# Three small edits at the seam between an output projection and a memory query projection: where two reciprocals stand, how eight decode rows are split, and where an exponential table is loaded

## The chip, the core and the metric

The kernel runs on one core of one Trainium2 chip. Such a core has five engines with their own instruction queues: TensorE (PE) multiplies matrices, with the loading of its stationary operand shown apart as PEld; VectorE (DVE), ScalarE (ACT) and GpSimd (POOL) work elementwise; SyncE (SP) here only starts transfers. The metric is device time in microseconds (us) of one execution of the whole program; the time of a kernel is the median of its runs.

## The reference

One inference step of a decoder layer, for a prompt of 1024 tokens and for 8 decode tokens that use the same weights, all in float32. What matters here is the end of the first part and the beginning of the second:

```python
# 1. hybrid mixer
a = head_rms(oa) * subln * (1.0 - lam_init)          # attention heads (group A)
r = head_rms(orr) * silu(gr)                         # retention heads (group B)
x = x + concatenate([a, r]) @ w_out
# 2. memory cross-attention
h = rmsnorm(x, g)                                    # g = norm_mem_q
q = (h @ w_mq)
p = softmax((q @ mk.T) * DH_M ** -0.5)
x = x + (p @ mv) @ w_mo
# 3. squared-ReLU MLP, then a final rmsnorm
```

`rmsnorm(x, g)` is `x / sqrt(mean(x*x) + eps) * g`. The decode tokens attend to a paged cache in part 1, so their rows of `oa` come by a way of their own.

## The kernel before

**Layout.** Activations lie transposed: 128 features on the partitions, tokens along the free dimension. The token columns are 1032 = 1024 prompt tokens and 8 decode tokens (`NT:T`), cut into three blocks of `CH` = 344. Blocks 0 and 1 are called the early tokens here, block 2 (688 to 1032, with the decode tokens) the late ones. The 1024 features make 8 tiles `kt`.

**Split products.** To keep float32 accuracy each operand is split into a high part, rounded by a conversion, and a low part, the rest. A product is three matmuls: high x high, high x low and low x high (`mm3`, line 80). The activations' parts lie in `UH` and `UL` ([128, 8, 1032]); those of a weight unit of 128 x 1024 in `wh` and `wl` (`unit`, line 135): a transfer into one of three `raw` buffers, the high part by a copy on ACT (line 129), the low part by a subtraction on DVE (line 130). There are four `wh` and four `wl` buffers. `split_gain` (line 143) does the same for activations and multiplies with the norm's gain: ACT at line 145 writes `UH`, DVE at line 146 writes `UL`.

**Output projection** (`proj_residual`, line 1479). It goes through the (feature tile, token block) pairs: first all of the early tokens, then the eight blocks (ft, 2). Each pair ends with an addition of the residual on DVE (line 1507, `x2`), a square on ACT (line 1562, the last at 1513) and an addition to a sum of squares on POOL (line 1563). The sums of the late tokens collect in `third` (a `raw` buffer, shown as `ssum_o`). Contraction runs over kt 4 to 7 (retention) first, then 0 to 3 (attention). Some blocks had half of their terms done earlier.

**Decode rows.** `decode_values` is a generator whose steps are taken between those blocks. Its last step transposes the 8 decode rows of the four attention heads into the PSUM tile `tr` (shown as `dtr`) and splits them into `UH` and `UL` columns 1024 to 1032 of kt 0 to 3, one head after the other (lines 1631 to 1636). The step before normalizes the rows in `oda` (the last instruction of it is line 1627). The late-token blocks need these columns.

**Norm of the query path.** `first_rstd` (line 1645) sums the squares of the early tokens over the partitions with a matmul and takes the root on ACT (line 1651) into `rb2`. Then `x2` is split with the gain `g_mq` into `UH` and `UL` for all 8 kt, first the early tokens, then the late ones (lines 1667 to 1669). The late ones overwrite columns that the last output blocks still read.

**Query projection** (from line 1735). Two reciprocals turn the roots in `rb2` into factors (line 1738), blocks 0 and 1. Then for each of four pairs of feature tiles two weight units are made (line 1740), and six blocks (f, c) of 24 matmuls each run, each scaled by `rb2` on the way out of PSUM (line 1767). Six PSUM banks hold such blocks. After the first block, (0, 0, 0), four pinned matmuls sum `third` over the partitions (tile `rs`); a root on ACT (line 1764) and a reciprocal on DVE (line 1765) make the late tokens' factors. Behind the query projection follow the memory keys and values and the attention, whose first exponential is at line 1889.

**What sets the order.** The program is not issued in the order of its text. A planner at build time takes, on each engine, what it believes ready, earlier lines first; the order on each engine is then fixed. Two things bind it: `pin[0]` keeps matmuls in the order of the text (line 64), and `with tc.issue_after(ins):` puts those instructions of its block that run on the engine of `ins` behind `ins`, without a wait of its own.

Of the kernel before, what the change touches and what calls it, by code (L numbers as in the profile page):

```python
# [10 lines left out]
F32 = mybir.dt.float32  # L11
# [37 lines left out]
def decoder_step(ctx: ExitStack, tc: tile.TileContext, i: dict, o: dict):  # L49
# [85 lines left out]
    def unit(u, parts=None, lo_engine=None, raw=None):  # L135
        return unit_of(lambda raw: [(raw[:, :1024], i["wall"][u])], f"u{u}", parts=parts, lo_engine=lo_engine, raw=raw)
# [1444 lines left out]
    with pool("x2") as XP:  # L1581
        x2 = [XP.tile([P, T], F32, tag=f"x2_{ft}", name=f"x2_{ft}") for ft in range(8)]
        g_mq = XP.tile([P, 8], F32, tag="g_mq", name="g_mq")
        nc.sync.dma_start(g_mq, i["g_mq"])
        with pool("c") as A:
            def decode_values():
                def dt(name):
                    return PB.tile([P, 512], F32, tag="av", name=name, bufs=1)

                acc = A.tile([P, T], F32, tag="dacc", name="dacc")  # L1590
                for k in range(8):
                    raw = A.tile([P, 1024], F32, tag="draw", name=f"cv_{k}", bufs=4)
                    gather(raw, i["cache_v"], idx, k)
                    with tc.issue_after(seen["DVE"]):
                        for x in range(8):
                            c = slice(x * P, x * P + P)
                            w = at[:, x % 4, 2 * k + x // 4 : 2 * k + x // 4 + 1]
                            if k == 0:
                                nc.vector.tensor_scalar(acc[:, c], raw[:, c], w, None, ALU.mult)
                            else:  # L1600
                                nc.vector.scalar_tensor_tensor(acc[:, c], raw[:, c], w, acc[:, c], ALU.mult, ALU.add)
                    yield
                vp = dt("vrep")
                mm(vp, selg, vdec, True, True)
                pd = A.tile([P, 1024], F32, tag="draw", name="pdv_8", bufs=4)
                nc.vector.tensor_mul(
                    pd[:, :512].rearrange("p (a v) -> p a v", v=P), vp.rearrange("p (a v) -> p a v", v=P),
                    at[:, :, 16:17].to_broadcast([P, 4, P]),
                )
                nc.vector.tensor_add(acc[:, :512], acc[:, :512], pd[:, :512])  # L1610
                yield

                with tc.issue_after(seen["PE"]):
                    op = dt("dop")
                    mm(op[:8, :], selgt, acc[:, 0:512], True, True)
                    mm(op[32:40, :], selgt, acc[:, 512:1024], True, True)
                    od2 = A.tile([P, 1024], F32, tag="draw", name="oda", bufs=4)
                    oda, sqd = od2[:8, 0:512], od2[:8, 512:1024]
                    nc.scalar.copy(oda, op[32:40, :])
                    nc.vector.tensor_add(oda, oda, op[:8, :])  # L1620
                    nc.vector.tensor_mul(sqd, oda, oda)
                    s4 = A.tile([8, 4], F32, tag="ds4", name="ds4")
                    nc.vector.tensor_reduce(s4, sqd.rearrange("p (h v) -> p h v", h=4), AX.X, ALU.add)
                    r4 = A.tile([8, 4], F32, tag="dr4", name="dr4")
                    rsqrt_small(r4, s4, 4, 1.0 / P, 8)
                    odv = oda.rearrange("p (h v) -> p h v", h=4)
                    nc.vector.tensor_mul(odv, odv, r4.unsqueeze(2).to_broadcast([8, 4, P]))
                yield
                yield
                with tc.issue_after(seen["PE"]):  # L1630
                    tr = dt("dtr")
                    for h in range(4):
                        nc.tensor.transpose(tr[:, h * 8 : h * 8 + 8], oda[:, h * P : h * P + P], ident[:8, :8])
                    odT = tr[:, :32].rearrange("p (k c) -> p k c", k=4)
                    for h in range(4):
                        split_gain(odT[:, h, :], subln8, h, NT, T, gcol=0)
                yield


            ssum = A.tile([P, T], F32, tag="ssum", name="ssum2")  # L1640
            early_tokens, late_tokens = slice(0, 2 * CH), slice(2 * CH, T)

            rb2s = []

            def first_rstd():
                rb2s.append(G.tile([P, T], F32, tag="rb2", name="rb2"))
                for c, (tag, n) in enumerate((("acc", 2), ("av", 1))):
                    cs = slice(c * CH, c * CH + CH)
                    f = PB.tile([P, 512], F32, tag=tag, name=f"rs_2_{c}", bufs=n)[:, :CH]
                    mm(f, ones.to_broadcast([P, P]), ssum[:, cs], True, True)  # L1650
                    nc.scalar.activation(rb2s[0][:, cs], f, AF.Sqrt, scale=1.0 / D, bias=half[:, 1:2])

            third = proj_residual(
                A, out_bank, U_OUT, OUT_KT, lambda ft: i["xT"][:, ft, :], lambda ft: x2[ft], ssum, "o", [us_out[x] for x in range(4)], decode_values(),
                [(ft, c) for ft in range(4) for c in range(2)] + [(4, 1), (7, 0)],
                lambda x: [
                    G.tile([P, 1024], F32R, tag="wl", name="wlo_3", bufs=RING) if (nm, x) == ("wl", 7)
                    else A.tile([P, 1024], F32R, tag=f"{nm}{x}", name=f"{nm}o_{x}") for nm in ("wh", "wl")
                ],
                first_rstd, ahead=len(OUT_EARLY), early=early_out, stage=([(4, 2)], [(5, 2), (6, 2)]), halved=OUT_HALVES,  # L1660
            )
            rb2 = rb2s[0]
            for ft in range(8):
                nc.gpsimd.dma_start(X2[ft], x2[ft])
        bc_ps.close()

        for lo, hi in ((0, 2 * CH), (2 * CH, T)):
            for kt in range(8):
                split_gain(x2[kt][:, lo:hi], g_mq, kt, lo, hi)

    pd_st = ExitStack()

    with pool("d") as A:
# [59 lines left out]
                    )  # L1733

        qm, dec = [], iter(())
        for c in range(2):
            cs = slice(c * CH, c * CH + CH)
            nc.vector.reciprocal(rb2[:, cs], rb2[:, cs])
        for pr in range(4):
            us = [unit(U_MQ + 2 * pr + x) for x in range(2)]  # L1740
            for f in range(2):
                qm.append(A.tile([P, T], F32, tag=f"qm{2 * pr + f}", name=f"qm_{2 * pr + f}"))

            late = [(0, 2), (1, 2)]
            rest = [(0, 0), (0, 1), (1, 0), (1, 1)]
            for f, c in late + rest if pr else rest + late:
                q = qm[2 * pr + f]
                cs = slice(c * CH, c * CH + CH)
                ps = PS.tile([P, 512], F32, tag="acc", name=f"mq_{pr}_{f}_{c}", bufs=6)
                pin[0] = (pr, f, c) == (0, 0, 0)  # L1750
                mm3(
                    ps[:, :CH],
                    [
                        (us[kt // 4][0][:, (kt % 4) * 256 + f * P : (kt % 4) * 256 + f * P + P],
                         us[kt // 4][1][:, (kt % 4) * 256 + f * P : (kt % 4) * 256 + f * P + P],
                         UH[:, kt, cs], UL[:, kt, cs])
                        for kt in range(8)
                    ],
                )
                if pin[0]:  # L1760
                    f = dt("rs_3")[:, :CH]
                    for x in range(2):
                        mm(f, ones.to_broadcast([P, P]), third[:, x * CH : x * CH + CH], x == 0, x == 1)
                    nc.scalar.activation(f, f, AF.Sqrt, scale=1.0 / D, bias=half[:, 1:2])
                    nc.vector.reciprocal(rb2[:, late_tokens], f)
                    pin[0] = False
                nc.vector.scalar_tensor_tensor(q[:, cs], ps[:, :CH], -1.0 / 16.0, rb2[:, cs], ALU.mult, ALU.mult)
                if c == 2:
                    nc.gpsimd.tensor_copy(qdm[:, 2 * pr + f, :], q[:, NT:])
                if (f, c) == (1, 2) and pr % 2:  # L1770
                    for _ in dec:
                        pass
                    dec = dec_scores(pr // 2)
                    continue
                for _ in range(3 if pr == 3 else 1):
                    next(dec, None)
# [984 lines left out]
```

## Time and profile before

| | |
|---|---|
| runs, median (lowest to highest) | 1479.63 us (1478.55 to 1484.31), 3 runs |
| profiled execution | 1479.72 us |
| its span, first to last instruction | 1478.0 us |
| mean granted clock of TensorE | 0.997 |
| loads of an activation table, whole span | 6, of 1.28 us each |

In the views of the trace a row of a timeline is: start and length in us, engine, line, operation, tile written <- tiles read, shape, count; a bracket gives how long the engine had been idle before and who released it. `UL<-x,g_mq,UH` is a low part of `x2`, `UL<-dtr,subln,UH` one of the decode rows, `rb<-rb` a reciprocal of the factors. Matmuls overlap: each lasts 0.32 us here, and one starts every 0.16 us. Idle time of an engine other than the bound one costs nothing by itself.

### The profile page before, as it was taken

To read this page: it belongs to the slowest core of one execution; us is meant where nothing else is said; L and a number is where in the kernel's file an instruction comes from. 1 tells how busy PE (TensorE), PEld (TensorE's weight loads), DVE (VectorE), ACT (ScalarE), POOL (GpSimd) and SP (SyncE) were. 2 spreads that over 40 slices of the span, in tenths; PEclk is the share of its full clock that TensorE was granted. 3 is DMA by queue.
4 is the path that set the end of the run, shared out by engine and by line. 5 is a ranking of instruction groups with operands and counts; after the bars stand their busy time and mean duration, and the time that the engine had idled before them with its cause. 6 is when DMAs were issued, how large, how long until landed. Compare 5 with 4: busy or idle time off the path is not lost.

```text
span 1478.0 us, 28131 instructions
## 1 busy us (share of the span) xinstructions
PE 1456.1 (99%) x11013; PEld 1400.9 (95%) x11013; DVE 1109.3 (75%) x2266; ACT 679.5 (46%) x1329; POOL 314.9 (21%) x345
## 2 busy tenths in 40 slices
PE   9999999999999999999999999999999999999998
PEld 7899779999889899989999999999999999999997
DVE  7666536888868765657877978888888888787876
ACT  7443435666542531257536534333434443343454
POOL 0034433122204621205022000000001311110380
PEclk9999999999999999999999999999999999999999
DMA  7255738216957175564582434334446674536273
GB/s 291 66 188 176 205 64 191 72 34 170 276 162 278 76 214 175 156 201 113 190 284 72 158 131 153 142 129 158 158 144 217 237 250 144 172 102 193 80 130 116
DMA packets 129833, 238.98 MB, mean 162 GB/s; under 512 B 13606, under 2 KB 80987, under 8 KB 129572
## 3 DMA queue, kind: packets, MB, share of 16 engines
q1 hardware_dynamic: 91354, 170.66, 36.1%
q0 software_dynamic: 27472, 46.93, 11.8%
q10 hardware_dynamic: 10874, 19.60, 3.5%
q8 instruction: 86, 1.41, 0.4%
q14 instruction: 47, 0.39, 0.1%
HBM read 171.13 MB, written 58.92 MB: 156 GB/s over the span
## 4 chain that ended last, share of the span: by engine, by line
PE 88%; DVE 6%; DMA 2%; ACT 2%; issue 1%; POOL 0%; SPq 0%; DVEq 0%; ACTq 0%
PE dn L2404 19%; PE Z L2236 9%; PE qkp L75 6%; PE Y L2236 6%; PE X L2236 6%; PE pr_m L75 6%; PE mq L75 6%; PE pr_o L75 4%; PE grp L75 3%; PE sp L75 2%; PE mk L75 2%; PE mv L75 2%; PE av L75 1%; PE mpv L75 1%; PE vap_z L524 1%; PE vrp_z L524 1%
## 5 line engine op out<-in xcount | busy, mean ns | idle before, releaser
L2404 PE MATMUL dn<-UH,wd 128*128 128x258 f32 (+1 forms) x1800 | 325.2, 283 | 1.5 <-ACT wd L2380 0.9
L2404 PEld LDWEIGHTS dn<-UH,wd 128*128 128x128 f32 x1800 | 278.6, 189 | 2.1 <-ACT wd L2380 1.0
L2404 PE MATMUL dn<-UL,wd 128*128 128x258 f32 x900 | 254.2, 282 | 0.0
L2404 PEld LDWEIGHTS dn<-UL,wd 128*128 128x128 f32 x900 | 170.0, 189 | 0.1
L2538 DVE TENSOR_TENSOR c<-c,dn 128x258 f32<-128x258 f32 (+1 forms) x217 | 88.7, 416 | 36.9 <-PE dn L2404 34.5
L2262 ACT ACTIVATE hq<-r 128x258 f32<-128x258 f32 x128 | 53.6, 420 | 119.2 <-DVE r L2261 119.2
L2236 PE MATMUL Z<-T_h,wu 128*128 128x258 f32 x512 | 98.2, 284 | 0.0
L2236 PE MATMUL X<-UH,wu 128*128 128x258 f32 x512 | 97.5, 282 | 0.0
L2380 ACT CAST wd<-raw_d 128x512 fp32r<-128x512 f32 x96 | 58.7, 619 | 78.9 <-PE dn L2404 74.1
L2044 ACT CAST wu<-raw_up 128x512 fp32r<-128x512 f32 x96 | 59.0, 615 | 60.0 <-PE Z L2236 50.0
L2373 ACT CAST UH<-raw_h 128x1032 fp32r<-128x1032 f32 x56 | 58.7, 1055 | 53.8 <-PE dn L2404 27.8
L2236 PEld LDWEIGHTS Z<-T_h,wu 128*128 128x128 f32 x512 | 81.4, 189 | 0.2 <-DVE u L2290 0.2
L2236 PEld LDWEIGHTS X<-UH,wu 128*128 128x128 f32 x512 | 81.4, 189 | 0.0
L2374 DVE TENSOR_TENSOR UL<-raw_h,UH 128x1032 fp32r<-128x1032 f32 x56 | 73.6, 1315 | 8.5 <-ACT UH L2373 8.5
L2381 DVE TENSOR_TENSOR wd<-raw_d,wd 128x512 fp32r<-128x512 f32 x96 | 72.1, 758 | 9.8 <-ACT wd L2380 9.6
L2273 POOL DMA_DIRECT2D HT<-ht x32 | 17.2, 536 | 292.4 <-DVE ht L2272 291.9
L129 ACT CAST wh_u<-raw_u 128x1024 fp32r<-128x1024 f32 x43 | 44.7, 1048 | 61.3 <-PE mq L75 39.0
L2236 PE MATMUL Z<-T_l,wu 128*128 128x258 f32 x256 | 72.4, 283 | 0.0
L2236 PE MATMUL X<-UL,wu 128*128 128x258 f32 x256 | 72.3, 283 | 0.0
L2045 DVE TENSOR_TENSOR wu<-raw_up,wu 128x512 fp32r<-128x512 f32 x96 | 64.7, 687 | 3.6 <-ACT wu L2044 3.6
L130 DVE TENSOR_TENSOR wl_u<-raw_u,wh_u 128x1024 fp32r<-128x1024 f32 x39 | 50.4, 1305 | 19.3 <-ACT wh_u L129 19.1
L75 PE MATMUL mq<-UH,wl_u 128*128 128x344 f32 x192 | 61.5, 320 | 2.1 <-DVE wl_u L130 2.1
(615 smaller groups left out, 4674.7 us busy)
## 6 DMA issues: line engine op xcount, KB each, us to landing
raw_u<-in_wall SPq DMA_DIRECT2D x49, 512.0 KB
HT<-ht POOLq DMA_DIRECT2D x32, 516.0 KB, 3.0
raw_h<-HT SPq DMA_DIRECT2D x32, 516.0 KB
raw_up<-in_wall SPq DMA_DIRECT2D x32, 512.0 KB
raw_d<-in_wall SPq DMA_DIRECT2D x32, 512.0 KB
HQ<-hq ACTq DMA_DIRECT2D x32, 387.0 KB
raw_h<-HQ SPq DMA_DIRECT2D x24, 516.0 KB
cmk<-in_cmk SPq DMA_DIRECT2D x16, 512.0 KB
```

The source lines that it names most:

```text
L75: pinned(nc.tensor.matmul(out, l, r, start=start, stop=stop))
L130: (lo_engine or nc.vector).tensor_sub(wl[:, :n], raw[:, :n], wh[:, :n].bitcast(F32))
L2044: nc.scalar.copy(w[:, :512], src)
L2045: nc.vector.tensor_sub(w[:, 512:], src, w[:, :512].bitcast(F32))
L2236: pinned(nc.tensor.matmul(ps, l, r[:, k, :], start=first and k == 0 and x == 0, stop=k == 3 and x == 2, skip_group_check=True))
L2262: nc.scalar.activation(h[:, PLACE[quad], :], r, AF.Square)
L2373: nc.scalar.copy(h, rv)
L2374: nc.vector.tensor_sub(l, rv, h.bitcast(F32))
L2380: nc.scalar.copy(w[:, :512], src)
L2381: nc.vector.tensor_sub(w[:, 512:], src, w[:, :512].bitcast(F32))
L2404: pinned(nc.tensor.matmul(ps[:, part], l, r[:, k, cq], start=first and k == 0 and x == 0, stop=k == 3 and x == 2, skip_group_check=True))
L2538: nc.vector.tensor_add(y, y, ps)
```

## The change

Three places are edited.

1. The decode rows: the four pairs of split instructions (one for each head) become one ACT and one DVE instruction over 4 x 8 columns. The DVE instruction is remembered as `seen["odT"]`, and of the early-token splits the DVE low parts of kt 4 to 7 are put behind it.
2. The two reciprocals of `rb2` move from ahead of the first weight units to behind them: behind the DVE low part of the second unit.
3. Right behind the root of the late tokens' sums, on ACT, a one-column exponential of a constant is written to a spare column of `third`. Its result is not used; it makes the exponential table the loaded one from there on.

```diff
@@ decode_values, last step
                     odT = tr[:, :32].rearrange("p (k c) -> p k c", k=4)
-                    for h in range(4):
-                        split_gain(odT[:, h, :], subln8, h, NT, T, gcol=0)
+                    nc.scalar.activation(UH[:, 0:4, NT:T], odT, AF.Copy, scale=subln8[:, 0:1])
+                    nc.vector.scalar_tensor_tensor(
+                        UL[:, 0:4, NT:T], odT, subln8[:, 0:1], UH[:, 0:4, NT:T].bitcast(F32), ALU.mult, ALU.subtract)
+                    seen["odT"] = nc.cur_bb.bb.instructions[-1]
                 yield
@@ splits of x2
         for lo, hi in ((0, 2 * CH), (2 * CH, T)):
             for kt in range(8):
-                split_gain(x2[kt][:, lo:hi], g_mq, kt, lo, hi)
+                with tc.issue_after(seen["odT"]) if not lo and kt > 3 else nullcontext():
+                    split_gain(x2[kt][:, lo:hi], g_mq, kt, lo, hi)
@@ query projection
         qm, dec = [], iter(())
-        for c in range(2):
-            cs = slice(c * CH, c * CH + CH)
-            nc.vector.reciprocal(rb2[:, cs], rb2[:, cs])
         for pr in range(4):
             us = [unit(U_MQ + 2 * pr + x) for x in range(2)]
+            if pr == 0:
+                seen["DVE"] = nc.cur_bb.bb.instructions[-1]
+                with tc.issue_after(seen["DVE"]):
+                    for c in range(2):
+                        cs = slice(c * CH, c * CH + CH)
+                        nc.vector.reciprocal(rb2[:, cs], rb2[:, cs])
...
                     nc.scalar.activation(f, f, AF.Sqrt, scale=1.0 / D, bias=half[:, 1:2])
+                    with tc.issue_after(nc.cur_bb.bb.instructions[-1]):
+                        nc.scalar.activation(third[:, 2 * CH : 2 * CH + 1], half[:, 0:1], AF.Exp)
                     nc.vector.reciprocal(rb2[:, late_tokens], f)
```

## The prediction

> **What bounds the kernel now.** Read in this order: the head of the page, the waits of PE, then the timelines of PE, DVE and ACT around the two waits that this change touches.
>
> ```profile
> span 1478.0 us, 28131 instructions
> PE 1456.1 (99%) x11013; PEld 1400.9 (95%) x11013; DVE 1109.3 (75%) x2266; ACT 679.5 (46%) x1329; POOL 314.9 (21%) x345
> ```
>
> TensorE bounds the whole span, so a microsecond counts only where PE stood idle. The waits of PE, whole span (who waited, for whom, us in total, times, longest):
>
> ```profile
> PE mq L75 <- DVE wl_u L130: 2.1, 1, 2.1
> ...
> PE pr_o L75 <- DVE UL L146: 1.4, 1, 1.4
> ```
>
> The reader is to see how small the stake is. PE's idle time in the whole span is 1478.0 - 1456.1 = 21.9 us, and the two waits around the change hold 2.1 + 1.4 of it.
>
> The first place, by the timelines of PE, ACT and DVE (start, length; in brackets the idle time before and its releaser):
>
> ```profile
> 499.74 0.90 PE L75 MATMUL pr_o<-UH,wh_u 128*128 128x344 f32 x4 [0.36 <-ACT UH L145]
> ...
> 502.51 0.43 PE L75 MATMUL pr_o<-UL,wh_u 128*128 128x344 f32 x1 [1.40 <-DVE UL L146]
> ```
> ```profile
> 499.42 0.27 ACT L145 ACTIVATE UH<-dtr,subln 128x8 fp32r<-128x8 f32 x1 [1.32 <-PE dtr L1633]
> 502.49 0.27 ACT L145 ACTIVATE UH<-dtr,subln 128x8 fp32r<-128x8 f32 x1 [2.80 <-DVE UL L146]
> ```
> ```profile
> 496.56 0.68 DVE L1627 TENSOR_TENSOR oda<-oda,dr 8x512 f32<-8x512 f32 x1 [0.73 <-POOL dr L141]
> 497.17 5.15 DVE L146 SCALAR_TENSOR_TENSOR UL<-x,g_mq,UH 128x688 fp32r<-128x688 f32 x6
> 502.25 0.21 DVE L146 SCALAR_TENSOR_TENSOR UL<-dtr,subln,UH 128x8 fp32r<-128x8 f32 x1
> ```
>
> ACT takes the first high part of the decode rows at 499.42, released by their transposes, and ends it at 499.69; but DVE is inside six low parts of the early tokens (5.15 us) and reaches the first decode low part only at 502.25. The last product blocks of the output projection need that low part.
>
> The second place is the start of the query products. DVE, then ACT, then PE:
>
> ```profile
> 511.30 2.29 DVE L1738 RECIPROCAL rb<-rb 128x344 f32<-128x344 f32 x1
> 513.51 0.45 DVE L1507 TENSOR_TENSOR x<-pr_o,x 128x344 f32<-128x344 f32 x1
> 513.88 2.29 DVE L1738 RECIPROCAL rb<-rb 128x344 f32<-128x344 f32 x1
> ...
> 517.62 1.22 DVE L130 TENSOR_TENSOR wl_u<-raw_u,wh_u 128x1024 fp32r<-128x1024 f32 x1
> 518.76 2.72 DVE L146 SCALAR_TENSOR_TENSOR UL<-x,g_mq,UH 128x344 fp32r<-128x344 f32 x2
> 521.41 0.50 DVE L1507 TENSOR_TENSOR x<-pr_o,x 128x344 f32<-128x344 f32 x1
> 521.83 2.52 DVE L146 SCALAR_TENSOR_TENSOR UL<-x,g_mq,UH 128x344 fp32r<-128x344 f32 x5
> 524.27 2.35 DVE L130 TENSOR_TENSOR wl_u<-raw_u,wh_u 128x1024 fp32r<-128x1024 f32 x2
> ```
> ```profile
> 512.61 1.05 ACT L129 CAST wh_u<-raw_u 128x1024 fp32r<-128x1024 f32 x1
> ...
> 516.52 0.58 ACT L145 ACTIVATE UH<-x,g_mq 128x344 fp32r<-128x344 f32 x1 [1.97 <-PE pr_o L75]
> ...
> 521.94 0.49 ACT L1513 ACTIVATE ssum_o<-x 128x344 f32<-128x344 f32 x1 [1.24 <-DVE x L1507]
> ```
> ```profile
> 519.62 0.32 PE L75 MATMUL mq<-UH,wh_u 128*128 128x344 f32 x1
> ...
> 525.54 0.42 PE L75 MATMUL mq<-UH,wl_u 128*128 128x344 f32 x1 [2.14 <-DVE wl_u L130]
> ...
> 527.22 1.32 PE L75 MATMUL rs<-ssum_o,ones 128*128 128x344 f32 x4
> ```
>
> And one row of the chain of work that ended last, for the pace of a query product, 44.64 / 284 = 0.157 us:
>
> ```profile
> 558.49 44.64 PE mq L75 x284
> ```
>
> Both weight high parts exist by 513.66 (the second is the row of 512.61), but DVE spends 4.58 us on two reciprocals and takes the low parts at 517.62 and 524.27. The second low part frees PE at 525.54.
>
> **The change part by part.** The sum is made against the profiled execution, 1479.72 us (span 1478.0 and 1.72 around it); the median of the runs shown is 1479.63.
>
> *Decode rows.* Four ACT and four DVE instructions of 8 columns become one each of 32 columns. The wide pair is not in the trace. For ACT, the nearest rows are 0.27 us at 8 columns and 0.58 at 344, so 32 columns lie between; I take 0.30. For DVE, the rows are 0.21 at 8 columns and 0.45 for an addition of 344 from PSUM; I take 0.26. The chain is then: high part 499.42 to 499.72, low part about 499.76 to 500.02. On DVE the planner must now put low parts 4 to 7 behind this. Ahead of it stand only low parts 2 and 3: 0 and 1 ran before the normalization at 496.56, and the six of 497.17 are 2 to 7. At 5.15 / 6 = 0.86 us each, two end at 498.9; DVE is free when the high part arrives. PE restarts at 499.74 as before, has 7 products that use only high parts (to 501.11, which is 502.51 less 1.40), and the low part comes 1.1 us before they are done. The 0.36 wait stays, the 1.40 wait goes: **-1.40 us** (between -1.0, should the row of 0.45 apply and the planner change the fill, and -1.76). The price is four low parts, 3.4 us, moved from 498.9 to about 500.0 to 503.4. Nothing on PE reads them before the query products at 518; next on DVE is the addition that began at 504.87, due 1.40 earlier, at 503.5. They fit, with 0.1 us over. An overrun would cost only the addition's start, which frees a PSUM bank, not PE's operand; I price it at nothing.
>
> *Reciprocals behind the first weights.* All that follows arrives 1.40 earlier: the second high part of the weights ready at 512.26 and the first before it, PE at the query products at 518.22. Between the additions DVE has only the two weight low parts (1.22 each) to do: the early low parts are done, and the late-token ones cannot start before 515.1, since their high parts wait for PE (row 516.52). So the first is done by about 512.3 and the second by 513.5 to 515, at the latest after one addition. PE needs the second low part first about 14 products into the query block, 14 x 0.157 = 2.2 us after 518.22, at 520.4. Cover: 5 us. The wait of 2.14 goes: **-2.14 us**. The reciprocals, 4.58 us, then run around 515 to 524, among eight late low parts of about 0.50 each. Who waits for them: the scaling of query block 0, which in PSUM holds one of six banks; at 24 x 0.157 = 3.8 us a block PE doesn't lack a bank for 22 us. Queued behind a reciprocal is also the addition of the last output block (row 521.41), whose square closes the sums that the pinned products at 527.22 read. With both stalls gone PE gets there at about 523.7; before, the sums stood at 522.43, and 1.40 earlier is 521.0. One reciprocal in between, 2.29, makes it 523.3: still in time. I price it at nothing, with 0 to 2.3 as bounds should both stand in front (521.0 + 4.58 - 523.7 = 1.9, and a POOL addition).
>
> *Table load behind the roots.* The ACT rows:
>
> ```profile
> 528.58 0.52 ACT L1764 ACTIVATE rs<-rs,half 128x344 f32<-128x344 f32 x1 [4.73 <-PE rs L75]
> 533.85 1.05 ACT L129 CAST wh_u<-raw_u 128x1024 fp32r<-128x1024 f32 x1 [4.75 <-DMA raw_u<-in_wall]
> ```
>
> and 120 us later, at the first exponentials:
>
> ```profile
> 650.63 1.28 ACT L1889 ACT_TABLE_LOAD   x1
> 652.55 0.45 ACT L1889 ACTIVATE ms<-ms,mmn 128x256 f32<-128x256 f32 x1 [0.64 <-DVE mmn L1885]
> ```
>
> Added: one load of 1.28 and an activation of one column (0.27 by the 8-column row, nearest) after 529.10, inside 4.75 us in which ACT waits for a weight transfer. Removed: the load at 650.63. It ended at 651.91 and ACT then waited 0.64 for DVE, so its removal moves nothing: **0** (bounds: 0 and -0.64, if DVE were re-ordered too). The new activation writes a spare column of the tile that holds the third sums. That tile is one of the three raw weight buffers, so its next transfer on SP's queue starts after the new write, some 2 us later than the pinned products would let it; but those run 3.5 earlier, so it is no later than now, and 0.
>
> The page ScalarE: Activation LUTs of the Trainium skill (What ACT_TABLE_LOAD costs) adds a drain of about 1.38 us to the load. By it the first exponential could not have started before 653.29 and the removal would be worth some 0.7 us, an estimate from that page; the trace has it at 652.55, 0.64 after the load, so the measurement decides against it and the sum stays.
>
> **Sum:** -1.40 - 2.14 + 0 = -3.54; 1479.72 - 3.54 = **1476.2 us**, which is 0.24% less. About 0.5% (7.4 us) is what a measurement of this kernel can tell from no change. Behind 525 the other engines follow PE's buffer releases and nothing of a fixed time stands in the list of PE's waits, so I take the gain to be kept to the end.
>
> **The rivals.**
>
> *Only one wait goes, chance 0.17.* The order on each engine is planned when the program is built, and the late low parts rank ahead of the weights, as the row of 521.83 before 524.27 shows. If the planner keeps the second weight low part behind them, only 1.40 is won: 1478.3. If it is the decode rows that stay late, 1477.6. Against it: late low parts can't start until about 515.1.
>
> *The clock comes too, chance 0.13.* Granted clock by windows (us; busy times; PEclk is the first number after POOL):
>
> ```profile
> 525.54:529.00 3.46, 3.46 (x18) 3.06 (x19) 1.60 (x2) 0.42 (x1) 0.32 (x1) 1.00 0.91 232
> 654.46:656.42 1.96, 0.01 (x2) 0.04 (x1) 1.56 (x5) 1.89 (x8) 0.00 (x0) 1.00 0.41 161
> 656.40:660.50 4.10, 4.08 (x22) 3.97 (x22) 3.19 (x8) 1.10 (x2) 0.00 (x0) 0.59 0.00 2
> ```
>
> The wait of 1.96 before 656.42 was followed by 4.1 us at 0.59, a loss of 4.10 x 0.41 = 1.7; the wait of 2.14 before 525.54 wasn't. If work shifted by 3.5 us escapes that dip, the time is 1476.2 - 1.7 = 1474.5; with the 0.64 of the table, 1473.9. The Trainium skill, TensorE: Matmul & The Clock Gate (The HAM clock gate), has the clock halve after an idle window of about 3.4 us, counted by a free-running window; by it no wait here is long enough and this rival would be void. The dip after 1.96 us speaks against that rule.
>
> *The gain is given back later, chance 0.10.* 3.5 us of earlier arrival meets a transfer, or the planner orders DVE worse before the first exponentials, where one more wait like 1.96 with its dip costs 3.7: 1479.9.
>
> *Slower, chance 0.08: the last output addition behind the reciprocals.* Suppose DVE does all it can before that addition: from about 515.1 the second weight part (1.22), both reciprocals (4.58), eight late low parts (4.0) and the third weight part (1.2). It then ends at 515.1 + 11.0 + 0.5 = 526.6 and its square at 527.1, while PE reaches the pinned products at 522.0 if it has no fill products (518.22 + 3.8). The wait is 5.1 us, and a dip like the one above comes with it: 1476.2 + 5.1 + 1.7 = 1483.0. It decides from a wait of 3.54 us on (addition ended after 525.05), or 1.84 if the clock dips. For it: a reciprocal is the longest DVE instruction there, and this addition already ran 1.8 us late behind other DVE work (PE's output block ended at 519.62, the addition began at 521.41). Against: it ranks ahead of the reciprocals whenever it is ready.
>
> **How the numbers follow.** The forecast has 0.52: both waits gone, 1475 to 1477.5. With one wait gone (1477.6 to 1478.3) and the clock (1473.9 to 1474.5) that is 0.82, so the range must reach from 1473.9 to 1478.3; the bounds of the costs (0.64 of the table and 0.36 of the first wait below; 2.3 of the pinned products above) widen it to **1473.0 to 1480.0**. Faster by over 0.5% means below 1472.2: only more than all priced gains, 0.05. Slower by over 0.5%, above 1487.1, takes more than the slow rival: 0.04. Within 0.5%: 0.91.
>
> **What would show it.** Right: on DVE two (not six) early low parts stand between the normalization and one decode low part near 500; no wait of PE for UL; both weight low parts before either reciprocal; no wait of mq for wl_u; a table load near 526 and none before the first exponential. Wrong: PE idle before the products of ssum_o (the pinned ones), late low parts ahead of the weights, or a new PE wait after 530 that eats 3.5 us.

## The result, and the profile after

The changed kernel takes 1472.90 us, the median of 8 runs (1471.88 to 1475.55), against 1480.17 for the kernel before in the same session (8 runs, 1478.55 to 1484.31). The ratio is 0.9951, with a 95% interval from 0.9939 to 0.9963: 7.3 us less, between 5.5 and 9.0. Forecast were 3.5 us less, 1476.2, with a range that ended at 1473.0. The head of the page after:

```profile
span 1473.4 us, 28129 instructions
PE 1455.7 (99%) x11013; PEld 1401.0 (95%) x11013; DVE 1107.9 (75%) x2263; ACT 679.7 (46%) x1327; POOL 314.4 (21%) x345
```

PE is as busy as before to 0.4 us; what fell is its idle time, from 21.9 to 17.7 us. The waits of PE, whole span:

```profile
PE dn L2412 <- DVE c L2546: 3.0, 2, 2.4
...
PE pr_o L75 <- ACT UH L1635: 0.4, 1, 0.4
...
PE mtr L78 <- DVE me L1901: 0.2, 1, 0.2
```

Both waits that the prediction wanted gone are gone. The third row is the surprise: the wait at the first transposes of the attention weights (tile `mtr`), 2.0 us before, is 0.2. (Most of the row at the top is one wait of 2.4 us at 1188 us, in the last projection. The clock dips behind it, so this span is only 4.6 shorter than before. A second profile of the same kernel, below, has neither, and a span of 1469.4.)

The decode rows in the timelines of ACT, DVE and PE:

```profile
499.24 0.29 ACT L1635 ACTIVATE UH<-dtr,subln 128x32 fp32r<-128x32 f32 x1 [1.03 <-PE dtr L1633]
```
```profile
494.91 0.68 DVE L1627 TENSOR_TENSOR oda<-oda,dr 8x512 f32<-8x512 f32 x1 [1.15 <-POOL dr L141]
495.52 0.92 DVE L146 SCALAR_TENSOR_TENSOR UL<-x,g_mq,UH 128x688 fp32r<-128x688 f32 x1
496.36 0.50 DVE L1507 TENSOR_TENSOR x<-pr_o,x 128x344 f32<-128x344 f32 x1
496.79 2.61 DVE L146 SCALAR_TENSOR_TENSOR UL<-x,g_mq,UH 128x688 fp32r<-128x688 f32 x3
499.56 0.25 DVE L1636 SCALAR_TENSOR_TENSOR UL<-dtr,subln,UH 128x32 fp32r<-128x32 f32 x1 [0.16 <-ACT UH L1635]
499.72 2.88 DVE L146 SCALAR_TENSOR_TENSOR UL<-x,g_mq,UH 128x688 fp32r<-128x688 f32 x3
```
```profile
499.57 0.74 PE L75 MATMUL pr_o<-UH,wh_u 128*128 128x344 f32 x3 [0.38 <-ACT UH L1635]
```

DVE is idle when the wide high part ends, takes the wide low part at once, and PE keeps only its wait of 0.38.

The start of the query products, DVE, then ACT and PE:

```profile
509.88 1.23 DVE L130 TENSOR_TENSOR wl_u<-raw_u,wh_u 128x1024 fp32r<-128x1024 f32 x1 [0.81 <-ACT wh_u L129]
511.03 0.51 DVE L1507 TENSOR_TENSOR x<-pr_o,x 128x344 f32<-128x344 f32 x1
511.45 1.54 DVE L130 TENSOR_TENSOR wl_u<-raw_u,wh_u 128x1024 fp32r<-128x1024 f32 x1
512.92 0.50 DVE L1507 TENSOR_TENSOR x<-pr_o,x 128x344 f32<-128x344 f32 x1
513.34 2.29 DVE L1746 RECIPROCAL rb<-rb 128x344 f32<-128x344 f32 x1
515.55 0.45 DVE L1507 TENSOR_TENSOR x<-pr_o,x 128x344 f32<-128x344 f32 x1
515.92 2.28 DVE L1746 RECIPROCAL rb<-rb 128x344 f32<-128x344 f32 x1
518.13 0.45 DVE L1507 TENSOR_TENSOR x<-pr_o,x 128x344 f32<-128x344 f32 x1
```
```profile
520.34 0.47 ACT L1513 ACTIVATE ssum_o<-x 128x344 f32<-128x344 f32 x1
...
523.44 1.28 ACT L1772 ACT_TABLE_LOAD   x1
524.73 0.20 ACT L1772 ACTIVATE ssum_o<-half 128x1 f32<-128x1 f32 x1
```
```profile
521.55 1.32 PE L75 MATMUL rs<-ssum_o,ones 128*128 128x344 f32 x4
```

Both weight low parts are done at 512.99, the reciprocals fill DVE behind them, and the last output addition follows the second reciprocal; its square ends at 520.81, 0.74 before PE comes to the pinned products, so PE loses nothing. The table load stands where it was put.

**Where the third gain comes from.** At the first exponentials the program is not changed, but the planned order of ACT is. In the kernel before (its first exponential, 652.55, is shown in the prediction) ACT, DVE and PE go on thus:

```profile
653.82 0.45 ACT L1889 ACTIVATE ms<-ms,mmn 128x256 f32<-128x256 f32 x1 [0.69 <-DVE mmn L1885]
```
```profile
651.84 0.68 DVE L1885 TENSOR_REDUCE mmn<-ms 128x2 f32<-128x512 f32 x1
...
654.50 0.69 DVE L1885 TENSOR_REDUCE mmn<-ms 128x2 f32<-128x512 f32 x1 [0.34 <-PE ms L75]
655.11 0.38 DVE L1891 RECIPROCAL msm<-msm 128x2 f32<-128x2 f32 x2
655.79 1.66 DVE L1893 TENSOR_SCALAR me<-ms,msm 128x256 f32<-128x256 f32 x4 [0.30 <-DVE msm L1891]
```
```profile
656.42 0.74 PE L78 MATMUL mtr<-ident,me 128*128 128x128 f32 x4 [1.96 <-ACT ms L1889]
```

and in the changed kernel:

```profile
648.17 0.45 ACT L1897 ACTIVATE ms<-ms,mmn 128x256 f32<-128x256 f32 x1 [2.19 <-DVE mmn L1893]
...
648.77 0.45 ACT L1897 ACTIVATE ms<-ms,mmn 128x256 f32<-128x256 f32 x1
```
```profile
647.46 0.68 DVE L1893 TENSOR_REDUCE mmn<-ms 128x2 f32<-128x512 f32 x1
...
649.37 0.17 DVE L1899 RECIPROCAL msm<-msm 128x2 f32<-128x2 f32 x1
```
```profile
650.25 0.74 PE L78 MATMUL mtr<-ident,me 128*128 128x128 f32 x4 [0.17 <-DVE me L1901]
```

The first score block has two halves, and its transposes need both. Before, the exponential at 653.82 is the first half of the second block (it waits for that block's minimum), and DVE takes a third minimum, which waits for PE, ahead of the reciprocals. After, both halves of the first block stand in a row. From the start of the first minimum (`mmn`) to that of the transposes it is 4.58 us before and 2.79 after.

The planned order of ACT's instructions, as the two programs have it (ms_0 is the first block, ms_1 the second; an x2 means both halves in a row):

```
before, ACT in order         changed, ACT in order
L1889 ACT_TABLE_LOAD         L1897 ACTIVATE ms_0  x2
L1889 ACTIVATE ms_0          L1897 ACTIVATE ms_1  x2
L1889 ACTIVATE ms_1          L1913 CAST mph_0
L1889 ACTIVATE ms_0
L1889 ACTIVATE ms_1
L1889 ACTIVATE ms_2  x2
L1905 CAST mph_0
```

### The profile page after: what moved, and what is told of

Its sections match the earlier page's. It is cut to its first block, busy times and chain, and to the rows that moved or that the text cites. A ratio compares the mean times of both kernels' runs of the same rounds, so it can differ in the third digit from the quotient of the medians.

```text
span 1473.4 us, 28129 instructions
## 1 busy us (share of the span) xinstructions
PE 1455.7 (99%) x11013; PEld 1401.0 (95%) x11013; DVE 1107.9 (75%) x2263; ACT 679.7 (46%) x1327; POOL 314.4 (21%) x345
## 4 chain that ended last, share of the span: by engine, by line
PE 88%; DVE 5%; DMA 2%; ACT 2%; issue 1%; POOL 0%; ACTq 0%; SPq 0%; DVEq 0%
PE dn L2412 20%; PE Z L2244 9%; PE qkp L75 6%; PE Y L2244 6%; PE X L2244 6%; PE mq L75 6%; PE pr_m L75 6%; PE pr_o L75 5%; PE grp L75 3%; PE sp L75 2%; PE mv L75 2%; PE mk L75 1%; PE av L75 1%; PE mpv L75 1%; PE vap_z L524 1%; PE vrp_z L524 1%
## 5 line engine op out<-in xcount | busy, mean ns | idle before, releaser
L2402 POOL TENSOR_TENSOR raw_d<-raw_d,raw_d 128x512 f32<-128x512 f32 x16 | 22.1, 1384 | 197.0 <-DVE raw_d L2398 145.3
```

## The experiments

Two theories at first. A: each edit pays at its own place, and the table edit pays at the first exponentials through the planned order. B: the wait of `mtr` went because everything arrives earlier. The first four kernels do one edit alone, or leave one out.

**The decode rows alone.**

Before, with the first edit:

```diff
-                    for h in range(4):
-                        split_gain(odT[:, h, :], subln8, h, NT, T, gcol=0)
+                    nc.scalar.activation(UH[:, 0:4, NT:T], odT, AF.Copy, scale=subln8[:, 0:1])
...
-                split_gain(x2[kt][:, lo:hi], g_mq, kt, lo, hi)
+                with tc.issue_after(seen["odT"]) if not lo and kt > 3 else nullcontext():
+                    split_gain(x2[kt][:, lo:hi], g_mq, kt, lo, hi)
```

> Before with the first edit alone: one wide split of the decode rows, four early low parts put behind it. Theory A (each edit pays at its own place, and the table edit pays at the first exponentials through the order planned there): the wait of pr_o for UL, 1.4 us, goes and PE reaches the first query product 1.4 to 1.7 us earlier; the wait of mtr for the exponentials stays near 2.0, with its dip of the clock; about -1.5 us in all. Theory B (the wait of mtr went because everything arrived earlier): mtr's wait shrinks here too, and the gain is over 3 us.

**The reciprocals alone.**

Before, with the second edit:

```diff
-        for c in range(2):
-            cs = slice(c * CH, c * CH + CH)
-            nc.vector.reciprocal(rb2[:, cs], rb2[:, cs])
...
+            if pr == 0:
+                seen["DVE"] = nc.cur_bb.bb.instructions[-1]
+                with tc.issue_after(seen["DVE"]):
...
+                        nc.vector.reciprocal(rb2[:, cs], rb2[:, cs])
```

> Before with the second edit alone: the two reciprocals behind the second weight low part. Theory A: the wait of mq for wl_u, 2.1 us, goes, that of pr_o for UL stays at 1.4, mtr's stays near 2.0 with its dip; -2.1 to -2.6 us. Theory B: mtr's wait shrinks with the earlier arrival, and the gain is over 4 us.

**The table edit alone.**

Before, with the third edit:

```diff
+                    with tc.issue_after(nc.cur_bb.bb.instructions[-1]):
+                        nc.scalar.activation(third[:, 2 * CH : 2 * CH + 1], half[:, 0:1], AF.Exp)
```

> Before with the third edit alone: the one-column exponential behind the root of the late sums. The planned order of the first exponentials already differs from before (both halves of the first block in a row). Theory A: mq's and pr_o's waits stay (2.1 and 1.4), mtr's wait falls from 2.0 to about 0.2 and the clock does not dip behind it; -3.3 us (1.8 and 1.6). Theory B: nothing arrives earlier, so mtr's wait stays near 2.0; 0 us.

**Without the table edit.**

The changed kernel, less the third edit:

```diff
-                    with tc.issue_after(nc.cur_bb.bb.instructions[-1]):
-                        nc.scalar.activation(third[:, 2 * CH : 2 * CH + 1], half[:, 0:1], AF.Exp)
```

> The changed kernel without the third edit: both other edits, the table loaded at the first exponential as before. Theory A: mq's and pr_o's waits gone, mtr's stays near 2.0, with or without a dip; -3.7 to -4.2 us against before. Theory B: mtr's wait falls as in the changed kernel; about -7 us.

What they and the later runs gave. The ratios are against runs of the kernel before on the same chip, with 95% intervals. The other columns are differences of starts in each kernel's one profile, in us: from the first decode transpose (`dtr`) to the first query product, from there to the decode transpose at the first scores (`dtp_m`), from the first minimum to the first transposes, and the wait of PE there.

| kernel | ratio | dtr to query | query to scores | mmn to mtr | wait of mtr |
|---|---|---|---|---|---|
| before | 1 | 20.65 | 129.14 | 4.58 | 1.96 |
| changed | 0.9951 (0.9939 to 0.9963) | 18.99 | 126.60 | 2.79 | 0.17 |
| decode rows alone | 0.9986 (0.9978 to 0.9995) | 19.01 | 131.46 | 4.16 | 2.08 |
| reciprocals alone | 0.9979 (0.9971 to 0.9988) | 20.66 | 126.59 | 4.17 | 1.55 |
| table edit alone | 0.9984 (0.9975 to 0.9992) | 20.24 | 131.26 | 2.79 | 1.13 |
| without the table edit | 0.9966 (0.9953 to 0.9979) | 19.01 | 126.61 | 4.23 | 1.60 |
| before, exponentials ordered | 0.9985 (0.9974 to 0.9996) | 20.65 | 129.16 | 3.06 | 0.44 |
| changed, old exponential order | 0.9955 (0.9941 to 0.9969) | 19.01 | 126.76 | 3.86 | 1.34 |
| without the table edit, ordered | 0.9946 (0.9931 to 0.9961) | 19.01 | 126.61 | 3.06 | 0.44 |
| changed, again | 0.9948 (0.9933 to 0.9962) | 19.02 | 126.61 | 2.79 | 0.30 |
| without the reciprocals | 0.9976 (0.9966 to 0.9985) | 19.01 | 129.51 | 2.80 | 0.17 |

Each edit has its own column, and the columns do not mix: the first is 19.0 only where the decode rows are split wide, the second 126.6 to 126.8 only where the reciprocals stand behind, and the chain is 2.8 with the table edit and 4.2 to 4.6 without it unless the exponentials are ordered by hand. The first column varies from run to run as well: over the four profiles of before that there are in the end it is 20.21, 20.65, 20.67 and 22.02. The 20.21, like the 20.24 with the table edit alone, has a wait of 0.9 us at `pr_o` in place of 1.4; the 22.02 has a dip of the clock.

In times the three alone give 2.1, 3.1 and 2.4 us (0.14, 0.21 and 0.16% of 1480), together 7.6, against 7.3 of the whole. Theory A holds. Of B little is left: the table edit alone, with nothing earlier, has the short chain, and both other edits together leave a wait of 1.60. That wait did move from 1.96 to 1.55 and 1.60 with the orders of ACT and DVE unchanged, by as much as the chain shrank (4.58 to 4.17 and 4.23). Why the chain shrank stays open, so a share of B is not shown. A's number for the table edit's wait, 0.2, was missed too: it is 1.13 in that run, with the same chain, because a weight transfer had come late and DVE began the first minimum later. Two of A's gains were short too, though inside the intervals: the reciprocals alone gave 3.1 us (1.8 to 4.3) where A had at most 2.6, and the kernel without the table edit 5.0 (3.1 to 7.0) where A had at most 4.2. And the second column of the first and third kernels is 2.2 larger than before's, which neither theory foresaw; that is the clock, below.

Is it the order, or the load itself that no longer stands in front? Two kernels part them.

**The order without moving the load.**

The kernel before, in the function that makes the scores:

```diff
             for x in range(2):
-                nc.scalar.activation(sp[:, x, :], sp[:, x, :], AF.Exp, bias=mn[:, x : x + 1], scale=-1.0,
-                                     accum_out=sm[:, x : x + 1])
+                with tc.issue_after(seen["exp"]) if (h, tp, x) in ((0, 0, 1), (0, 1, 0), (0, 1, 1)) else nullcontext():
+                    nc.scalar.activation(sp[:, x, :], sp[:, x, :], AF.Exp, bias=mn[:, x : x + 1], scale=-1.0,
+                                         accum_out=sm[:, x : x + 1])
+                if h == 0:
+                    seen["exp"] = nc.cur_bb.bb.instructions[-1]
```

> Before with none of the three edits, but with the four exponentials of the first two score blocks put in the order of the text (first block's two halves, then the second's); the table is still loaded ahead of the first of them. If the order is what the table edit bought: the chain from the first minimum (mmn) to the first transposes (mtr) falls from 4.6 us to 2.8 to 3.0, as in the run with the table edit alone (2.79), the load stays hidden ahead of it, and the gain is that of the table edit alone, 1.5 to 2.5 us. If the load itself is what cost: the chain stays above 4 us and the time that of before.

Its ACT and PE rows:

```profile
650.03 1.28 ACT L1890 ACT_TABLE_LOAD   x1
652.09 0.45 ACT L1890 ACTIVATE ms<-ms,mmn 128x256 f32<-128x256 f32 x1 [0.78 <-DVE mmn L1885]
```
```profile
654.43 0.74 PE L78 MATMUL mtr<-ident,me 128*128 128x128 f32 x4 [0.44 <-DVE me L1896]
```

The load still stands ahead of the first exponential and ends, at 651.31, 0.78 us before it; the wait of PE falls to 0.44 all the same, and the kernel gains 2.2 us (0.6 to 3.8).

**The old order without the load.**

The changed kernel, where the second half of block (0, 0) is held back; `exp` makes one exponential and remembers it, `finish` the reciprocals and products behind them:

```diff
...
+            if (h, tp) == (0, 0):
+                exp(0)
+                seen["rest"] = exp, finish
+            elif (h, tp) == (0, 1):
+                with tc.issue_after(seen["exp"]):
+                    exp(0)
+                exp_0, finish_0 = seen["rest"]
+                with tc.issue_after(seen["exp"]):
+                    exp_0(1)
+                with tc.issue_after(seen["exp"]):
+                    exp(1)
+                finish_0()
+                finish()
...
```

> The changed kernel, its table load moved as there, but the four exponentials forced into the order that before has (first block's first half, second block's first half, first block's second half, second block's second half). If the order is the cause: the chain from mmn to mtr is 0.6 to 1.8 us longer than the 2.79 of the changed kernel, the wait of mtr comes back at 0.8 to 2.0 us, and the kernel is 0.7 to 2 us slower than the changed one. If the load is the cause: 2.8 and no wait.

```profile
650.98 0.74 PE L78 MATMUL mtr<-ident,me 128*128 128x128 f32 x4 [1.34 <-DVE me L1904]
```

Without any load in the way the wait is back at 1.34 and the chain 1.07 longer. Only ACT's order is forced here; on DVE the third minimum stays behind the first block's products. So 1.07 us is the part of ACT's order. The third minimum ahead of the reciprocals, as in before, is likely the rest, but no run moved it alone. In time its median is 1.5 us above that of the changed kernel in the same session, but the two intervals overlap widely, so here the profile decides, not the times.

**Both other edits, with the exponentials ordered by hand and the load unmoved.**

The changed kernel, less the third edit, and with the exponentials chained as above:

```diff
-                        nc.scalar.activation(third[:, 2 * CH : 2 * CH + 1], half[:, 0:1], AF.Exp)
...
+                with tc.issue_after(seen["exp"]) if (h, tp, x) in ((0, 0, 1), (0, 1, 0), (0, 1, 1)) else nullcontext():
...
```

> The changed kernel without the third edit, but with the exponentials of the first two score blocks in the order of the text. If the order is all that the third edit buys: chain 2.8 to 3.0, wait of mtr under 0.5, time within 1 us of the changed kernel, about -7 us against before. If the load costs too: between the kernel without the third edit (-5.0) and the changed one.

It is not to be told from the changed kernel: 1472.94 us against 1472.44 for the next one in the same session. Beyond the order nothing of the third edit is seen. No run beat the changed kernel by more than its interval.

**The changed kernel again.** Nothing is edited.

> The changed kernel once more, unaltered. Its waits of PE around the three edits are as in its first profile (none for UL, none for wl_u, mtr 0.2), -7.3 us against before. If the dips of the granted clock belong to fixed places of the program, they lie at 1188 us again; if they fall where a wait meets a free-running window, they lie elsewhere or are absent.

The waits around the three edits are those of the first profile (`mtr` 0.30). The dip of the clock that the first had at 1188 us is absent, and so is the wait of 2.4 us ahead of it.

**The kernel before again, three times, and the second edit left out.** The three are unedited; the fourth is the changed kernel with:

```diff
+        for c in range(2):
+            cs = slice(c * CH, c * CH + CH)
+            nc.vector.reciprocal(rb2[:, cs], rb2[:, cs])
...
-            if pr == 0:
-                seen["DVE"] = nc.cur_bb.bb.instructions[-1]
...
-                        nc.vector.reciprocal(rb2[:, cs], rb2[:, cs])
```

> Before, unaltered, a second profile, for the clock alone. The three places sum to 5.8 us, the measured gain is 7.3. If the rest is dips of the granted clock that follow the two longest waits removed or shortened (mq for wl_u 2.1, mtr 2.0), then repeated profiles of before show a dip behind one of the two in about half of the cases, each worth 1.5 to 2.2 us, and not always behind the same one. If dips have nothing to do with these waits, they lie elsewhere here, as often as in the changed kernel.

> The same, third profile of before: a dip behind mq's or mtr's wait in about half of the cases.

> The same, fourth profile of before: a dip behind mq's or mtr's wait in about half of the cases.

> The changed kernel without the second edit: decode rows and table edits, reciprocals ahead of the weights. By the places: the wait of mq stays at 2.1 to 2.4 (first query product to first memory scores 129.1 us, or 131.3 with a dip of the clock), transposes to first query product 19.0, chain to mtr 2.8 us; 3.3 us under before in all. If the second edit changes the other two places, one of these numbers differs.

Windows from the restart of PE behind `mtr` in the second, third and fourth profile of before, then in the kernel with the decode rows alone (busy times as before; the granted clock is the first number behind POOL's):

```profile
658.63:662.83 4.20, 4.20 (x22) 4.07 (x23) 3.17 (x8) 1.10 (x2) 0.00 (x0) 0.60 0.02 6
```
```profile
655.52:659.32 3.80, 3.80 (x23) 3.67 (x24) 3.17 (x8) 1.10 (x2) 0.00 (x0) 0.67 0.03 6
```
```profile
660.23:664.07 3.84, 3.84 (x22) 3.71 (x23) 3.17 (x8) 1.10 (x2) 0.00 (x0) 0.67 0.03 6
```
```profile
655.57:658.29 2.72, 2.72 (x22) 2.59 (x23) 2.43 (x7) 1.39 (x4) 0.00 (x0) 1.00 0.01 3
```

The same 22 or 23 matmuls take 3.8 to 4.2 us in place of 2.7. From the first `mtr` to the first product of the next kind (`mpv`) it is 6.00 us in each of the four profiles of before and 4.46 to 4.50 in the ten others, so the dip costs 1.5 us each time. In all four profiles of before (the first is in the prediction) the clock dips behind this wait. It does not after 2.08 us of the same wait in the last row. Behind the wait of `mq`, which is 2.1 to 2.4 us in the eight profiles that have it, the clock dips in three (1.4 us in one of before, 2.2 in the kernels with the decode rows and the table edit alone), and behind the 1.4 us of `pr_o` in one profile of before (22.02 in place of 20.65 us in the first column's stretch). Of the 15 dips inside the spans of the 14 profiles that makes eight; one stands behind the wait at 1188 us, and six lie elsewhere (391.85 and 425.98 in the fourth profile of before, 390.84 and 424.97 without the table edit, 769.12 with the reciprocals alone, 775.54 with the table edit alone). So "about half", expected for the waits of `mq` and `mtr` in before, was not a good number: one of the two had a dip in all four profiles.

The stretches above are wider than a dip. The clock record has only full and half speed, and every one of the 15 dips lasts 3.41 us at half speed. In each profile the changes of the clock lie whole multiples of this length apart (before: 657.13, 660.54 and 1472.91, the last 238 lengths of 3.413 us after the second). Windows laid on these marks tell the cases apart; two are of the first profile of before, then two of the kernel with the decode rows alone:

```profile
653.72:657.13 3.41, 1.46 (x13) 1.15 (x12) 2.67 (x9) 2.54 (x10) 0.00 (x0) 1.00 0.49 163
657.13:660.54 3.41, 3.41 (x19) 3.41 (x18) 2.46 (x6) 1.10 (x2) 0.00 (x0) 0.50 0.00 0
```
```profile
651.54:654.95 3.41, 1.95 (x17) 1.75 (x15) 3.03 (x9) 2.70 (x10) 0.00 (x0) 1.00 0.96 326
654.95:658.36 3.41, 2.79 (x23) 2.69 (x24) 3.12 (x10) 1.98 (x6) 0.00 (x0) 1.00 0.02 10
```

In before the wait of 1.96 us, 654.46 to 656.42, lies whole in one window, and the next has half the clock. With the decode rows alone the wait of 2.08, 653.49 to 655.57, is cut at 654.95, and no dip follows. Over the 14 profiles, from the first mark to the last instructions, all eight windows in which PE stood idle for 1.95 us or more were followed by a dip, and none of the five with 1.5 to 1.9; the five waits of `mq` without a dip were all cut by a mark. The other seven dips follow windows with 0.26 to 1.46 us idle; what made those stays open. If the marks fall anywhere with equal chance, a wait of 1.96 us lies whole in a window in (3.41 - 1.96) / 3.41 of the cases, some four in ten. By this estimate four of four is luck, and the mean price of the dip at `mtr` is 0.6 us and not 1.5.

Leaving out the second edit gives 3.6 us (2.2 to 5.0), with the places at 1.64 + 1.79 = 3.4, and the other two places are as in the changed kernel.

## Why the prediction was wrong

**The decode rows: right, and slightly short.** The wide pair took 0.29 and 0.25 us against 0.30 and 0.26; the low part was ready at 499.81, and the wait of 1.40 went. The stretch shrank by 1.64, not 1.40. A wait in the list begins at the modelled end of a matmul, 0.16 us after the next could have started, and the product behind the first one starts 0.26 us later, not 0.16 (502.51 and 502.77 in before); so each wait costs some 0.25 us more than its row. One statement was wrong without harm: not two but four early low parts stand between the normalization and the decode low part, since the planner took the normalization first.

**The reciprocals: right, and short by the same.** Low parts at 509.88 and 511.45, reciprocals behind. It gave 2.54 us in place of 2.14: 0.26 by the same reading of a wait, and 0.14 that I can't place. The rival with the last output addition did not come: it ran behind the second reciprocal, but PE had 0.74 us left. The nine fill products are gone, as that rival had it.

**The table load: this step failed.** The prediction read that the load "ended at 651.91 and ACT then waited 0.64 for DVE, so its removal moves nothing". For the chip that is true: with the load in place and the order changed by hand, the gain is there; with the load gone and the order kept, the wait is. But moving the load also moved the plan: in every program built with the load in front of the first exponential the planned order interleaves the two blocks, and in the three built with it elsewhere and nothing forced (the changed kernel, the table edit alone, and without the reciprocals) it does not. That is worth 1.79 us at this place, 7.66 us from the scores to the transposes in before and 5.87 after. The rows were there: the exponential behind the first one waited for another block's minimum. I took the order behind the load as given, and as the most that another order could give, the 0.64. With both other edits in place the chain falls from 4.23 to 2.79, so there it is worth 1.44.

**The clock: the right mechanism as a rival, with the wrong weight.** The prediction gave the dip behind `mtr` a chance of 0.13 to go, as luck of a shifted start, at 1.7 us. It went because its wait went. It cost 1.5 us in all four profiles of before, so a part of it belonged into the price of the wait. By the places the sum is 1.64 + 2.54 + 1.79 = 6.0 us; with this dip 7.5, with the mean price estimated above 6.6, against 7.3 measured. The interval of the whole (5.5 to 9.0) holds all three, so that the rest is the dip is argued from the profiles, not shown by the times. Times of the parts speak against the full 1.5: the reciprocals alone have 2.55 + 0.42 by the places, 4.5 with the whole dip, and gave 3.1 (1.8 to 4.3); the kernel without the reciprocals has 3.4, 4.9 with it, and gave 3.6 (2.2 to 5.0).

The Trainium skill's page TensorE: Matmul & The Clock Gate (The HAM clock gate) would have voided that rival: as the prediction read it, it has the clock halve after an idle window of about 3.4 us. Here a window of 3.41 us with 1.95 us idle was enough, eight times of eight. That the window runs freely, as the page also says, agrees with the wait of `mq`: three dips in eight, each where the wait lay whole in a window.

**The range.** It ended at 1473.0, 0.1 us above the median. It took in a dip or the table's 0.64, but no case in which the table edit won a wait of PE. The 0.64 is in it twice, since the 1473.9 that it widens has it already; counted once the range ends at 1473.5. And the 0.5% that the prediction took as the least that a measurement tells from no change was too much: the interval of the eight runs is 0.12% either way.

## What to carry to other kernels

Where a planner sets the order of the queues, an edit that costs the chip nothing still can change the plan elsewhere; look at what stands in which order around every wait of the bounding engine that the moved instruction precedes, not at whether the instruction itself is hidden. Price a short wait of TensorE with more than its row: some 0.25 us of restart, and a dip of the clock, 1.5 us here, times the share of runs in which it falls there, for which four profiles were too few here. For gains of a few tenths of a per cent, stretches between fixed instructions of one profile tell edits apart that times of a dozen runs don't.

## What the runs showed of the hardware

The clock went to half speed for 3.41 us, 15 times in 14 profiles, at marks whole multiples of 3.41 us apart. It did so after each of the eight windows between marks in which PE was idle for 1.95 us or more, and after seven with 0.26 to 1.46. The 0.6 to 0.7 over some 4 us in the rows above is the mean of such a dip and of full speed around it. Behind the wait of 2.4 us at 1188 us, in the first profile of the changed kernel:

```profile
1188.26:1192.00 3.74, 3.74 (x21) 3.74 (x22) 3.00 (x7) 0.00 (x0) 0.00 (x0) 0.62 1.03 385
```

What made the dips after less idle time was not settled. The table load put behind the root left no pause: the load of 523.44 ends at 524.72, and the exponential starts at 524.73.
